# One decoder layer on one core: the memory's keys and values projected first, x made ready beside them

## The chip, the core and the metric

The kernel runs on one core of a Trainium2 chip. The metric is device microseconds (us) from start to end of one execution. The engines are PE (TensorE, matrix products and transposes), DVE (VectorE), ACT (ScalarE), POOL (GpSimd) and SP (SyncE, which here only issues DMAs). Engines run their own instruction queues in order and wait for each other by semaphores.

## What is computed

One hybrid decoder layer on 256 rows of width 2048, in float32. Cut to what matters here:

```python
x = x + 0.5 * swiglu_ffn(rmsnorm(x, g_ffn1), w_ffn1_gu, w_ffn1_down)      # d_ff 5632
h = rmsnorm(x, g_mix)
conv_in, cq, ckv, k_pe, mq, gate_logits = split(h @ w_in)
y_a = silu(layernorm(causal_conv31(glu(conv_in)))) @ w_conv_out
y_b = latent_attention(cq, ckv, k_pe) @ w_mla_out                         # 12 heads
mk, mv = split(rmsnorm(mem, g_mem) @ w_mem_kv, 2)                         # mem (256, 2048), 2 x 1024 columns
mk = rmsnorm(mk per head); mq = rmsnorm(mq per head)                      # 4 heads of 256
y_c = (softmax(mq mk^T / 16) mv) @ w_mem_out
x = x + (gates * (y_a, y_b, y_c)).sum() @ w_out
x = x + 0.5 * swiglu_ffn(rmsnorm(x, g_ffn2), w_ffn2_gu, w_ffn2_down)
```

The memory's keys and values depend on `mem`, `g_mem` and `w_mem_kv` alone, on nothing that the layer computes from x.

## The kernel before, in words

**Products.** Float32 is split into a high part of type fp32r and the rest: weights into `h` and `l` (`wh`, `wl` in the mixer), activations into `tH` and `tL` (plain), `xN` or `xsH`, `xsL` (forms). One product of tiles is three matmuls (`mul`, L497 to L499): high by high, low by high, high by low. The split of a weight chunk is a cast on ACT (L468, L199 in the mixer) and a subtraction on DVE (L469, L201).

**FFN stage.** The weights come in chunks of two K tiles by 2 x 512 columns (`pair_chunk`, L456: one chunk is 1 MB, two loads of 512 KB on SP's queue, three buffers in turn). Eight pairs make a block of gate and up (`PAIRS`). A plain pair (`eight`) takes eight tile products, 24 matmuls of 512 columns. In a block with forms, the pairs 0, 2 and 4 (`SEVEN`) take seven products, 21 matmuls, by a Strassen-like scheme: DVE adds weight tiles (L486), splits three more tiles (`t`, `th`, `tl`), and the activations need sums too (`seven_forms`, L505 to L507). `run_pairs` (L580) walks a list of such units, asks for the next chunk ahead, and calls a hook after each. A block's four sums stay in the four PSUM banks `acc`; four more banks (`misc`) hold transposes and the seven scheme's remainders.

**The start.** x comes in four blocks of 512 columns (`load_x`). The first block of gate and up is plain: x is turned with its gain but not its row norm (`block_T`, transposes at L270, tH at L252, tL at L253), and the norm is applied to the result. Meanwhile the squares of x are summed on ACT (L242), and after the fourth pair on, `prepare` scales x by its row norm (L632), turns it again (`pair_forms`, L527) and makes the forms for the other ten blocks. The hooks `mid` and `after` place these steps. Only the first chunk is loaded and split in four small pieces (`first`).

**The mixer.** `mixer` projects conv_in, then latents, rotary key and memory query from `w_in`, and then the memory's keys and values from `w_mem_kv` (`linear`, same three matmuls at L220 to L222): four column blocks of 16 K tiles, 384 matmuls of 512 columns. `memory_T` (L1070) loads the memory by POOL's queue, turns it and sums its squares shortly before. Then come the memory's attention (`mem_attention`, four heads in steps `turn`, `scores`, `probs`, `values` spread over the first gate blocks), the latent attention and the rest. The convolution is 360 steps on DVE (L1022); they fill what DVE has free.

**Order.** Steps that are not pinned are placed on each engine's queue by the framework's scheduler, by its own estimates; `pinned` steps keep the program's order, and until the first four units are through, so do the loads (`pin_dma`). `defer` holds a step back by a count of weight chunks, `until` and `flush` call it earlier.

Of the kernel before, what the change touches and what calls it, by code (L numbers as in the profile page):

```python
# [19 lines left out]
P = 128  # L20
# [56 lines left out]
class Layer:  # L77
    def __init__(self, ctx, tc, d, out):
# [14 lines left out]
        self.begin = True  # L93
# [362 lines left out]
    def pair_chunk(self, W3, pr, cs, seven, first=False):  # L456
# [123 lines left out]
    def run_pairs(self, units, after, end=None):  # L580


        def chunk(n):
            _, pr, seven, _, W3, cs, _ = units[n]
            w = self.pair_chunk(W3, pr, cs, seven, self.begin)
            self.begin = False
            return w

        w = chunk(0)
        for n, (q, pr, seven, forms, W3, cs, last) in enumerate(units):  # L590
# [11 lines left out]
            after(n, q)  # L602
# [10 lines left out]
    def ffn(self, W, blocks, xs, gain, rstd_, W_down, load, done, mid=None, between=None, end=None):  # L613
# [3 lines left out]
        get = self.xT_fn(blocks)  # L617

        def plain_forms(pr):
            r = []  # L620
            for k in range(2):
                h, l = get(2 * pr + k)
                r.append([(h[:, tt * P:tt * P + P], l[:, tt * P:tt * P + P]) for tt in range(2)])
            return r

        forms = {}

        def prepare(c):
            rstd = self.get(rstd_)
            xn = xs[c]  # L630
# [18 lines left out]
        units = []  # L649
        for b in range(NB):  # L650
            cs = slice(b * CB, (b + 1) * CB)
            if b == 0:
                q = self.lazy(lambda: self.quad(PAIRS, 0))
                units += [(q, pr, False, plain_forms, W3, cs, pr == PAIRS - 1) for pr in range(PAIRS)]
            else:
                q = self.lazy(lambda: self.quad(PAIRS - N7, N7))
                units += [(q, pr, pr in SEVEN, forms.__getitem__, W3, cs, pr == PAIRS - 1) for pr in range(PAIRS)]

        def after(n, q):
            b, pos = divmod(n, PAIRS)  # L660
            if b == NB:
                return down(pos, q)
            if b > NB:
                return down(n - NB * PAIRS, q)
            if b == 0:
                if mid is not None:
                    mid(pos)
                if PAIRS - 5 <= pos < PAIRS - 1:
                    prepare(pos - (PAIRS - 5))
# [6 lines left out]
            if b == 0:  # L676
# [19 lines left out]
            self.defer(4.0 * 6 - 1, lambda: turn(h))  # L696

# [627 lines left out]
```

## Time and profile before

| | |
|---|---|
| three runs | 2416.39, 2417.24, 2417.72 us; median 2417.24 |
| profiled execution | 2419.43 us, from its first to its last instruction (span) 2417.7 us |
| PE busy | 2396.8 us, 99% of the span |
| DVE busy | 1878.0 us, 78% |
| ACT busy | 1271.8 us, 53% |
| chain that ended last | 96% PE, 2% DVE, 1% ACT, 1% DMA |
| granted TensorE clock | 0.998 of full speed on average |

The busy time of PE counts the length of a matmul in the pipeline, so a stretch can read as busy while matmuls start late; counting instructions against the time of a stretch tells more. The chain is followed back from the last instruction, at each step to what released it.

### The profile page before, as it was taken

Reading aid. Unit: us, or ns where it says so; the run is one execution under the profiler, and the core shown is the slowest. Engines: PE = TensorE matmul, PEld = TensorE weight load, DVE = VectorE, ACT = ScalarE, POOL = GpSimd, SP = SyncE. Lnnn points to the kernel's source line nnn. Section 1 sums busy time; section 2 is a strip of 40 time slices with the busy share of each in tenths; the row PEclk is TensorE's granted clock in tenths of the full one; section 3 lists DMA queues with packets and bytes.
Section 4 is the critical chain, followed back from the end, with each engine's and each line's share of the span. In section 5 each row is a group of like instructions: output and inputs, shape, how many; then the busy total and the mean of one; then the engine's idle time right before and its main releaser. Section 6 shows DMA issues by size and latency. Waiting matters only on the chain.

```text
span 2417.7 us, 29511 instructions
## 1 busy us (share of the span) xinstructions
PE 2396.8 (99%) x10938; PEld 1987.0 (82%) x10938; DVE 1878.0 (78%) x2130; ACT 1271.8 (53%) x1452; POOL 84.2 (3%) x185
## 2 busy tenths in 40 slices
PE   8999999999999999999999999999999999999999
PEld 6788888888888889888888788888888888888887
DVE  5898888898875999975555576665688888888985
ACT  6655555455554555544556565345655555555543
POOL 1000000000000000000112100000000000000000
PEclk9999999999999999999999999999999999999999
DMA  6556555566567665664555557756555655566664
GB/s 221 175 184 212 200 197 195 205 218 217 193 221 234 184 185 181 183 195 139 172 162 164 166 174 218 235 183 205 195 192 192 206 194 194 205 204 215 207 201 149
DMA packets 224513, 469.94 MB, mean 194 GB/s; under 512 B 16304, under 2 KB 24096, under 8 KB 224368
## 3 DMA queue, kind: packets, MB, share of 16 engines
q1 hardware_dynamic: 218192, 449.90, 57.4%
q0 software_dynamic: 4992, 16.04, 2.0%
q10 hardware_dynamic: 1184, 2.11, 0.2%
q8 instruction: 86, 1.41, 0.2%
q14 instruction: 59, 0.48, 0.1%
HBM read 461.69 MB, written 6.29 MB: 194 GB/s over the span
## 4 chain that ended last, share of the span: by engine, by line
PE 96%; DVE 2%; ACT 1%; DMA 1%; issue 1%; SPq 0%; DVEq 0%; ACTq 0%
PE acc L498 15%; PE acc L497 15%; PE acc L499 15%; PE acc L220 12%; PE acc L222 12%; PE acc L221 12%; PE misc L497 3%; PE misc L499 3%; PE misc L498 3%; DVE l L469 1%; PE misc L645 1%; PE misc L270 1%; ACT h L468 1%; PE misc L1253 1%; PE misc L1252 0%
## 5 line engine op out<-in xcount | busy, mean ns | idle before, releaser
L468 ACT CAST h<-raw 128x2048 fp32r<-128x2048 f32 (+1 forms) x267 | 505.1, 1892 | 525.4 <-PE acc L498 274.8
L469 DVE TENSOR_TENSOR l<-raw,h 128x2048 fp32r<-128x2048 f32 (+1 forms) x267 | 604.6, 2265 | 190.9 <-ACT h L468 190.4
L201 DVE TENSOR_TENSOR wl<-raw,wh 128x1024 fp32r<-128x1024 f32 (+1 forms) x330 | 397.3, 1209 | 226.4 <-ACT wh L199 223.2
L199 ACT CAST wh<-raw 128x1024 fp32r<-128x1024 f32 (+1 forms) x330 | 342.7, 1042 | 389.8 <-PE acc L221 339.0
L497 PE MATMUL acc<-h,xN 128*128 128x512 f32 x1312 | 513.0, 391 | 0.0
L499 PE MATMUL acc<-l,xN 128*128 128x512 f32 x1312 | 511.1, 390 | 0.0
L498 PE MATMUL acc<-h,xN 128*128 128x512 f32 x1312 | 511.0, 389 | 0.0
L220 PE MATMUL acc<-wh,tH 128*128 128x512 f32 (+3 forms) x1088 | 422.2, 388 | 0.5 <-DVE gate L994 0.5
L222 PE MATMUL acc<-wl,tH 128*128 128x512 f32 (+3 forms) x1088 | 415.9, 382 | 0.0
L221 PE MATMUL acc<-wh,tL 128*128 128x512 f32 (+3 forms) x1088 | 415.4, 382 | 0.0
L499 PEld LDWEIGHTS acc<-l,xN 128*128 128x128 f32 x1312 | 246.4, 188 | 51.1
L497 PEld LDWEIGHTS acc<-h,xN 128*128 128x128 f32 x1312 | 246.5, 188 | 50.2
L498 PEld LDWEIGHTS acc<-h,xN 128*128 128x128 f32 x1312 | 246.5, 188 | 50.1
L220 PEld LDWEIGHTS acc<-wh,tH 128*128 128x128 f32 x1088 | 204.6, 188 | 39.6 <-issue 2.6
L222 PEld LDWEIGHTS acc<-wl,tH 128*128 128x128 f32 x1088 | 204.4, 188 | 38.8
L221 PEld LDWEIGHTS acc<-wh,tL 128*128 128x128 f32 x1088 | 204.8, 188 | 36.6
L486 DVE TENSOR_TENSOR t<-raw 128x1024 f32<-128x1024 f32 (+1 forms) x168 | 160.5, 955 | 14.3 <-DMA raw<-in_w_ffn_down_dram 9.3
L469 DVE TENSOR_TENSOR tl<-t,th 128x1536 fp32r<-128x1536 f32 x84 | 147.3, 1754 | 7.0 <-ACT th L468 4.5
L1022 DVE SCALAR_TENSOR_TENSOR y<-aT,cw,y 128x256 f32<-128x256 f32 x360 | 150.3, 476 | 0.0
L468 ACT CAST th<-t 128x1536 fp32r<-128x1536 f32 x84 | 124.8, 1486 | 43.4 <-PE acc L498 30.2
L497 PE MATMUL misc<-th,xsH 128*128 128x512 f32 x168 | 65.9, 392 | 3.8 <-ACT xf L530 3.8
L497 PE MATMUL misc<-h,xsH 128*128 128x512 f32 x168 | 66.5, 396 | 0.9 <-ACT xf L530 0.9
(287 smaller groups left out, 2765.6 us busy)
## 6 DMA issues: line engine op xcount, KB each, us to landing
raw<-in_w_ffn_gu_dram SPq DMA_DIRECT2D x290, 512.0 KB, 4.0
raw<-in_w_in_dram SPq DMA_DIRECT2D x172, 512.0 KB, 3.6
raw<-in_w_ffn_down_dram SPq DMA_DIRECT2D x152, 512.0 KB, 4.5
raw<-in_w_ffn_gu_dram SPq DMA_DIRECT2D x124, 256.0 KB, 4.0
raw<-in_w_mem_kv_dram SPq DMA_DIRECT2D x32, 512.0 KB, 3.8
raw<-in_w_out_dram SPq DMA_DIRECT2D x32, 512.0 KB, 3.6
raw<-in_w_ffn_down_dram SPq DMA_DIRECT2D x48, 256.0 KB, 4.8
raw<-in_w_conv_out_dram SPq DMA_DIRECT2D x24, 512.0 KB, 4.6
```

The source lines that it names most:

```text
L199: self.pinned(nc.scalar.copy(wh, raw))
L201: self.pinned(nc.vector.tensor_tensor(out=wl, in0=raw, in1=wh.bitcast(F32), op=ALU.subtract))
L220: nc.tensor.matmul(ps[tt], xh[:, t], wh[:, j, :], start=st, stop=False)
L221: nc.tensor.matmul(ps[tt], xl[:, t], wh[:, j, :], start=False, stop=False)
L222: nc.tensor.matmul(ps[tt], xh[:, t], wl[:, j, :], start=False, stop=sp)
L468: self.pinned(nc.scalar.copy(h[:, r], src[:, r]))
L469: self.pinned(nc.vector.tensor_tensor(out=l[:, r], in0=src[:, r], in1=h[:, r].bitcast(F32), op=ALU.subtract))
L486: add = lambda o, x, y: nc.vector.tensor_tensor(out=o, in0=x, in1=y, op=ALU.add)
L497: nc.tensor.matmul(ps, xh, wh, start=st, stop=False)
L498: nc.tensor.matmul(ps, xl, wh, start=False, stop=False)
L499: nc.tensor.matmul(ps, xh, wl, start=False, stop=sp)
L1022: nc.vector.scalar_tensor_tensor(out=y, in0=aT[ch // 3][:, ch % 3, k:k + S], scalar=self.cw[:, ch, k:k + 1], in1=y, op0=ALU.mult, op1=ALU.add)
```

## The change

The program now begins with the memory: `load_in` brings its four blocks, `turn_m` turns them with g_mem, and two plain runs of eight pairs (`plain_run`), keys then values, project it with the FFN stage's chunks and hooks (`mem_unit`). The result is scaled by the memory's row norm and written to DRAM (`kvd`); the keys' squares are summed at once. The four blocks of x are loaded after pairs 3 to 6 of the keys, their squares summed, and the forms of x are made after pairs 1, 3, 5 and 6 of the values. All eleven blocks of the first gate and up then use forms (`mixed_run`), so three of eight pairs in the first block are seven-product units; the second FFN keeps its plain first block. In the mixer, `memory_T` and the projection are gone; four loads on POOL's queue bring the keys and values back. The first chunk is still loaded and split in quarters; the second to the sixth are loaded as before and split in halves (`step`).

```diff
-    def pair_chunk(self, W3, pr, cs, seven, first=False):
+    def pair_chunk(self, W3, pr, cs, seven, step=4):
...
-                if first:
+                if step == 1:
                     for g in range(2):
                         self.pinned(nc.sync.dma_start(out=raw[:, 2 * i + g], in_=W3[k, g, cs]), self.pin_dma)
                 else:
                     self.pinned(nc.sync.dma_start(out=raw[:, 2 * i:2 * i + 2], in_=W3[k, :, cs]), self.pin_dma)
-            return split(raw, "hl", 4, 1 if first else 4)
+            return split(raw, "hl", 4, step)
...
-            _, pr, seven, _, W3, cs, _ = units[n]
-            w = self.pair_chunk(W3, pr, cs, seven, self.begin)
-            self.begin = False
-            return w
+            _, pr, seven, _, W3, cs, _, _ = units[n]
+            self.begun += 1
+            return self.pair_chunk(W3, pr, cs, seven, 1 if self.begun == 1 else 2 if self.begun < 7 else 4)
 
         w = chunk(0)
-        for n, (q, pr, seven, forms, W3, cs, last) in enumerate(units):
+        for n, (q, pr, seven, forms, W3, cs, last, after) in enumerate(units):
...
             w = nxt
             self.tick(4.0)
-            after(n, q)
+            after(q)
+
+    def plain_run(self, W3, cs, blocks, after):
+
+        get = self.xT_fn(blocks)
+
+        def forms(pr):
+            r = []
+            for k in range(2):
+                h, l = get(2 * pr + k)
+                r.append([(h[:, tt * P:tt * P + P], l[:, tt * P:tt * P + P]) for tt in range(2)])
+            return r
+
+        q = self.lazy(lambda: self.quad(PAIRS, 0))
+        return [(q, pr, False, forms, W3, cs, pr == PAIRS - 1, lambda q, pr=pr: after(pr, q)) for pr in range(PAIRS)]
+
+    def mixed_run(self, W3, cs, forms, after):
+        q = self.lazy(lambda: self.quad(PAIRS - N7, N7))
+        return [(q, pr, pr in SEVEN, forms.__getitem__, W3, cs, pr == PAIRS - 1,
+                 lambda q, pr=pr: after(pr, q)) for pr in range(PAIRS)]
+
+    def prepare(self, forms, xs, c, gain, rstd_):
+
+        rstd = self.get(rstd_)
+        for tt in range(2):
+            self.nc.scalar.activation(out=xs[c][:, tt], in_=xs[c][:, tt], func=AF.Identity, scale=rstd[:, tt:tt + 1])
+        for pr in (2 * c, 2 * c + 1):
+            forms[pr] = self.pair_forms(xs[c], pr, gain, pr in SEVEN)
 
     def lazy(self, make):
         got = []
...
+        mem_v = d["mem"].rearrange("(t p) c -> p t c", p=P)
+        ms, memT, xs, forms = [], [], [], {}
+        rmem, rstd = {}, {}
+        self.kvd = [self.dp.tile([P, 2, CB], F32, tag=f"kv{c}", name=f"kv{c}") for c in range(NCB)]
+        self.ssk = self.const([P, 2, 2, 2], name="ssmk")
+
+        def load_in(to, v, c):
             x = self.gen([2, CB], F32, "x")
-            n = CB // 2 if c == 0 else CB
+            n = CB // 2 if to is ms and c == 0 else CB
             for o in range(0, CB, n):
-                self.pinned(nc.sync.dma_start(out=x[:, :, o:o + n], in_=x_v[:, :, c * CB + o:c * CB + o + n]), True)
-            xs.append(x)
-
-        def turn_x(c):
-            blocks.append(self.block_T(xs[c], self.gains("g_ffn1", c), 0.0, 0.1))
-
-        def mid(pos):
+                self.pinned(nc.sync.dma_start(out=x[:, :, o:o + n], in_=v[:, :, c * CB + o:c * CB + o + n]), True)
+            to.append(x)
+
+        def turn_m(c):
+            memT.append(self.block_T(ms[c], lambda j: self.g_mem[:, 4 * c + j:4 * c + j + 1], 0.0, 0.1))
+
+        def mem_unit(g, pos, q):
+            n = PAIRS * g + pos
             self.pin = False
-            self.pin_dma = pos < 4
-            if pos < 3:
-                load_x(pos + 1)
-            if pos in (0, 2, 4):
-                turn_x(pos // 2 + 1)
-            if pos == 2:
-                self.stats(xs, D, 0.1, 0.1, True, rstd)
-
-        (self.g_ffn1,) = self.load_gains([d["g_ffn1"]], "g1", nc.scalar)
-        load_x(0)
-        turn_x(0)
+            self.pin_dma = n < 4
+            if n < 3:
+                load_in(ms, mem_v, n + 1)
+            if n in (0, 2, 4):
+                turn_m(n // 2 + 1)
+            if n == 2:
+                self.stats(ms, D, 0.1, 2.0, True, rmem)
+            if 3 <= n < 3 + NCB:
+                load_in(xs, x_v, n - 3)
+            if n == 6:
+                self.stats(xs, D, 0.1, 2.0, True, rstd)
+            if n in (9, 11, 13, 14):
+                self.prepare(forms, xs, {9: 0, 11: 1, 13: 2, 14: 3}[n], self.g_ffn1, rstd)
+            if pos < PAIRS - 1:
+                return
+            r = self.get(rmem)
+            kv = []
+            for c in range(2):
+                t = self.gen([2, CB], F32, "mkv")
+                kv.append(t)
+                for tt in range(2):
+                    nc.scalar.activation(out=t[:, tt], in_=q["F"][2 * c + tt], func=AF.Identity,
+                                         scale=r[:, tt:tt + 1])
+                nc.gpsimd.dma_start(out=self.kvd[2 * g + c], in_=t)
+            if g == 0:
+                for h in range(MEM_HEADS):
+                    self.defer(4.0 + 4 * h, lambda h=h: self.head_sumsq(self.ssk, kv, h))
+
+        self.g_ffn1, self.g_mem = self.load_gains([d["g_ffn1"], d["g_mem"]], "g1", nc.scalar)
+        load_in(ms, mem_v, 0)
+        turn_m(0)
+        W3 = d["w_mem_kv"].rearrange("k (h g f) -> k h g f", h=2, g=2)
+        units = []
+        for g in range(2):
+            units += self.plain_run(W3[:, g], slice(0, CB), memT, lambda pos, q, g=g: mem_unit(g, pos, q))
...
-        self.ffn(d["w_ffn1_gu"], blocks, xs, self.g_ffn1, rstd, d["w_ffn1_down"],
-                 residual(lambda c: x_v[:, :, c * CB:(c + 1) * CB]), done1, mid,
-                 (self.load_mixer, self.setup_mixer), end1)
+        units += self.ffn(d["w_ffn1_gu"], forms, d["w_ffn1_down"], residual(lambda c: x_v[:, :, c * CB:(c + 1) * CB]),
+                          done1, between=(self.load_mixer, self.setup_mixer))
+        self.run_pairs(units, end1)
...
-        memT, rmem = self.memory_T()
...
         kv = []
-        ssk = self.const([P, 2, 2, 2], name="ssmk")
-        for c in range(4):
-            ps = self.linear(d["w_mem_kv"], c * CB, CB, self.xT_fn(memT), KT)
-            r = self.get(rmem)
+        for c in range(NCB):
             t = self.gen([2, CB], F32, "mkv")
+            nc.gpsimd.dma_start(out=t, in_=self.kvd[c])
             kv.append(t)
-            for tt in range(2):
-                nc.scalar.activation(out=t[:, tt], in_=ps[tt], func=AF.Identity, scale=r[:, tt:tt + 1])
-            if c < 2:
-                for h in (2 * c, 2 * c + 1):
-                    self.defer(1.0 + h % 2, lambda h=h: self.head_sumsq(ssk, kv, h))
         self.flush()
-        omT = self.mem_attention(mq, kv[:2], kv[2:], ssq, ssk)
+        omT = self.mem_attention(mq, kv[:2], kv[2:], ssq, self.ssk)
 
         oT = [{"h": self.gen([4, S], F32R, "oH"), "l": self.gen([4, S], F32R, "oL"), "left": 0} for _ in range(3)]
         merged = [None] * NCB
...
+        units = []
+        for b in range(NB):
+            cs = slice(b * CB, (b + 1) * CB)
+            then = lambda pos, q, b=b: after(b, pos, q)
+            if b == 0 and blocks is not None:
+                units += self.plain_run(W3, cs, blocks, then)
+            else:
+                units += self.mixed_run(W3, cs, forms, then)
+
```

How the instructions lie now, at three places. **SP, the loads after the third chunk.** `raw` are weight chunks (two loads each), `x` blocks of x or, from `in_mem`, of the memory. Before:

```order
L479 DMA raw_257<-in_w_ffn_gu_dram 128x2x512 x2
L772 DMA x_288<-in_x_dram 128x2x512
L479 DMA raw_302<-in_w_ffn_gu_dram 128x2x512 x2
L479 DMA raw_394<-in_w_ffn_gu_dram 128x2x512 x2
L479 DMA raw_466<-in_w_ffn_gu_dram 128x2x512 x2
```

With the change:

```order
L479 DMA raw_267<-in_w_mem_kv_dram 128x1024 x2
L778 DMA x_300<-in_mem_dram 128x2x512
L479 DMA raw_314<-in_w_mem_kv_dram 128x1024 x2
L479 DMA raw_420<-in_w_mem_kv_dram 128x1024 x2
L778 DMA x_364<-in_x_dram 128x2x512
L479 DMA raw_366<-in_w_mem_kv_dram 128x1024 x2
L479 DMA raw_468<-in_w_mem_kv_dram 128x1024 x2
L479 DMA raw_553<-in_w_mem_kv_dram 128x1024 x2
L479 DMA raw_502<-in_w_mem_kv_dram 128x1024 x2
```

`raw_366` is the sixth chunk, `raw_420` the seventh: the seventh is issued first, with a block of x between them; the ninth and tenth (`raw_502`, `raw_553`) are exchanged too.

**ACT, the first casts.** `h` are the casts of weight chunks, `tH` the turned activations, two K tiles from each `misc`. Before:

```order
L252 ACTIVATE tH_124<-misc_126,g_17_119 128x256 x2
L468 CAST h_148<-raw_143 128x512 x4
L468 CAST h_165<-raw_162 128x2048
L252 ACTIVATE tH_124<-misc_193,g_17_119 128x256
L468 CAST h_218<-raw_215 128x2048
L252 ACTIVATE tH_124<-misc_193,g_17_119 128x256
```

With the change:

```order
L252 ACTIVATE tH_130<-misc_132,g_18_125 128x256 x2
L468 CAST h_154<-raw_149 128x512 x4
L468 CAST h_171<-raw_168 128x1024 x2
L252 ACTIVATE tH_130<-misc_201,g_18_125 128x256
L468 CAST h_226<-raw_223 128x1024 x2
L252 ACTIVATE tH_130<-misc_201,g_18_125 128x256
```

The second and third chunks (`h_171`, `h_226`) are cast in halves; the third and fourth K tile's tH keep their places behind them.

**DVE, one head of the memory's attention.** `mx`, `nmx`, `rs` and `me` are its softmax, `wl` weight splits, `y` steps of the convolution. Before:

```order
L1132 TENSOR_REDUCE mx_8239<-misc_8234 128x2
L1134 TENSOR_TENSOR nmx_8241<-mx_8239,mnsq_8105 128x2
L1141 RECIPROCAL rs_8247<-sm_8244 128x2
L1143 TENSOR_SCALAR me_8243<-me_8243,rs_8247 128x256 x2
L201 TENSOR_TENSOR wl_8400<-raw_8396,wh_8398 128x1024
```

With the change:

```order
L1142 TENSOR_REDUCE mx_8282<-misc_8277 128x2
L1043 SCALAR_TENSOR_TENSOR y_6188<-aT_6184,cw_1572,y_6188 128x256
L1144 TENSOR_TENSOR nmx_8284<-mx_8282,mnsq_8003 128x2
L1043 SCALAR_TENSOR_TENSOR y_6188<-aT_6184,cw_1572,y_6188 128x256
L1043 SCALAR_TENSOR_TENSOR y_6188<-aT_6185,cw_1572,y_6188 128x256
L1043 SCALAR_TENSOR_TENSOR y_6189<-aT_6185,cw_1572,y_6189 128x256 x2
L1151 RECIPROCAL rs_8290<-sm_8287 128x2
L1043 SCALAR_TENSOR_TENSOR y_6189<-aT_6186,cw_1572,y_6189 128x256
L1153 TENSOR_SCALAR me_8286<-me_8286,rs_8290 128x256 x2
L201 TENSOR_TENSOR wl_8434<-raw_8430,wh_8432 128x1024
```

Before, the convolution was through ahead of this; now six of its steps lie between the steps of the softmax.

## Rows read from the trace of the kernel before

**Rows 1.** The page: busy us, share and instructions of each engine
```profile
PE 2396.8 (99%) x10938; PEld 1987.0 (82%) x10938; DVE 1878.0 (78%) x2130; ACT 1271.8 (53%) x1452; POOL 84.2 (3%) x185
```

**Rows 2.** Two stretches: engines' busy time, PE clock, DMA share, GB/s
```profile
core 0: us, PE busy (x) PEld busy (x) DVE busy (x) ACT busy (x) POOL busy (x), PEclk, DMA share, GB/s
149.40:191.80 42.40, 42.40 (x192) 35.20 (x191) 37.93 (x33) 22.16 (x16) 0.00 (x0) 1.00 0.59 199
880.00:1060.00 180.00, 180.00 (x900) 153.77 (x899) 175.73 (x331) 98.83 (x165) 9.04 (x12) 1.00 0.61 185
```

**Rows 3.** The chain of waits, in order of time: start us, us, what
```profile
150.51 0.88 PE misc L645 x8
```

**Rows 4.** Stretch from third chunk to hidden block, columns as above
```profile
26.80:106.78 79.98, 72.34 (x330) 57.67 (x329) 60.12 (x64) 57.31 (x81) 8.53 (x17) 0.98 0.48 163
```

**Rows 5.** PE's transposes in that stretch: xcount, busy us, mean ns
```profile
L527 PE MATMUL misc<-ident,x 128*128 128x128 f32 x32 | 4.8, 275 | 0.0
...
L270 PE MATMUL misc<-ident,x 128*128 128x128 f32 x19 | 3.1, 275 | 1.7 <-ACT xf L530 1.7
```

**Rows 6.** Waits of PE in that stretch: total us, times, longest us
```profile
PE misc L497 <- ACT xf L530: 4.2, 2, 3.8
```

**Rows 7.** Two stretches of 10 us, columns as in rows 2
```profile
10.00:20.00 10.00, 7.18 (x27) 5.14 (x27) 2.69 (x3) 4.21 (x4) 0.00 (x0) 0.88 1.03 385
...
50.00:60.00 10.00, 7.12 (x36) 5.15 (x35) 9.78 (x14) 9.46 (x19) 5.75 (x12) 1.00 0.69 231
```

**Rows 8.** The timeline: start us, us, instruction [idle before <-releaser]
```profile
13.95 1.90 ACT L468 CAST h<-raw 128x2048 fp32r<-128x2048 f32 x1 [5.01 <-DMA raw<-in_w_ffn_gu_dram]
...
15.33 0.66 PE L270 MATMUL misc<-ident,x 128*128 128x128 f32 x4 [0.92 <-DMA x<-in_x_dram]
15.75 0.47 ACT L252 ACTIVATE tH<-misc,g 128x256 fp32r<-128x256 f32 x1
...
18.07 1.90 ACT L468 CAST h<-raw 128x2048 fp32r<-128x2048 f32 x1 [1.85 <-DMA raw<-in_w_ffn_gu_dram]
18.09 0.48 DVE L253 SCALAR_TENSOR_TENSOR tL<-misc,g,tH 128x256 fp32r<-128x256 f32 x1
...
26.82 0.48 PE L497 MATMUL acc<-h,tH 128*128 128x512 f32 x1
```

**Rows 9.** DVE and ACT, 0 to 110 us: xcount, busy us, mean ns
```profile
L469 DVE TENSOR_TENSOR l<-raw,h 128x2048 fp32r<-128x2048 f32 x16 | 36.7, 2291 | 18.2 <-ACT h L468 18.2
...
L632 ACT ACTIVATE x<-x,r 128x512 f32<-128x512 f32 x8 | 5.3, 722 | 0.0
...
L469 DVE TENSOR_TENSOR tl<-t,th 128x1536 fp32r<-128x1536 f32 x3 | 5.3, 1754 | 1.0 <-ACT th L468 1.0
...
L486 DVE TENSOR_TENSOR t<-raw 128x1024 f32<-128x1024 f32 x4 | 4.9, 1222 | 0.0
...
L250 DVE TENSOR_TENSOR xN<-xf,xN 128x512 fp32r<-128x512 f32 x5 | 3.4, 687 | 0.7 <-ACT xN L249 0.7
...
L505 DVE TENSOR_TENSOR xf<-xf 128x256 f32<-128x256 f32 x3 | 1.3, 424 | 0.5 <-ACT xf L530 0.5
...
L506 DVE TENSOR_TENSOR xf<-xf 128x128 f32<-128x128 f32 x3 | 0.9, 288 | 0.0
```

**Rows 10.** Page: costliest groups (busy, mean ns), weights' issues (us to landing)
```profile
L201 DVE TENSOR_TENSOR wl<-raw,wh 128x1024 fp32r<-128x1024 f32 (+1 forms) x330 | 397.3, 1209 | 226.4 <-ACT wh L199 223.2
L199 ACT CAST wh<-raw 128x1024 fp32r<-128x1024 f32 (+1 forms) x330 | 342.7, 1042 | 389.8 <-PE acc L221 339.0
...
L1022 DVE SCALAR_TENSOR_TENSOR y<-aT,cw,y 128x256 f32<-128x256 f32 x360 | 150.3, 476 | 0.0
...
raw<-in_w_ffn_gu_dram SPq DMA_DIRECT2D x290, 512.0 KB, 4.0
```

**Rows 11.** The timeline of one head's softmax in the memory's attention
```profile
1074.28 0.62 DVE L1143 TENSOR_SCALAR me<-me,rs 128x256 f32<-128x256 f32 x2
...
1078.24 0.60 PE L1151 MATMUL misc<-ident,me 128*128 128x128 f32 x4
```

More of the change, by code (lines that the diff above doesn't have):

```diff
@@ L92, in __init__ @@
         self.pin = True
-        self.begin = True
+        self.begun = 0
     def ffn_stage(self):
@@ L359, in setup_mixer @@
         nc, d = self.nc, self.d
-        (self.g_mix, self.g_ffn2, self.g_mem, self.ln_g, self.ln_b, self.cv_b, self.g_q_a, self.g_kv_a,
+        (self.g_mix, self.g_ffn2, self.ln_g, self.ln_b, self.cv_b, self.g_q_a, self.g_kv_a,
          gqn, gkn, gmq, gmk) = self.turn_rows(*self.rows, "gains")
@@ L578, in remainders, with run_pairs @@
         v.tensor_tensor(out=e[1][:, 1], in0=e[1][:, 0], in1=p7, op=ALU.add)
-    def run_pairs(self, units, after, end=None):
+    def run_pairs(self, units, end=None):
         def chunk(n):
-            _, pr, seven, _, W3, cs, _ = units[n]
-            w = self.pair_chunk(W3, pr, cs, seven, self.begin)
-            self.begin = False
-            return w
+            _, pr, seven, _, W3, cs, _, _ = units[n]
+            self.begun += 1
+            return self.pair_chunk(W3, pr, cs, seven, 1 if self.begun == 1 else 2 if self.begun < 7 else 4)
         w = chunk(0)
-        for n, (q, pr, seven, forms, W3, cs, last) in enumerate(units):
+        for n, (q, pr, seven, forms, W3, cs, last, after) in enumerate(units):
             q, f = q(), forms(pr)
@@ L611, in lazy, with ffn @@
         return get
-    def ffn(self, W, blocks, xs, gain, rstd_, W_down, load, done, mid=None, between=None, end=None):
+    def ffn(self, W, forms, W_down, load, done, blocks=None, xs=None, gain=None, rstd_=None, between=None):
         nc = self.nc
         W3 = W.rearrange("k (g f) -> k g f", g=2)
[L617 to L630, printed above, removed]
-            for tt in range(2):
-                nc.scalar.activation(out=xn[:, tt], in_=xn[:, tt], func=AF.Identity, scale=rstd[:, tt:tt + 1])
-            for pr in (2 * c, 2 * c + 1):
-                forms[pr] = self.pair_forms(xn, pr, gain, pr in SEVEN)
         hT = []
@@ L648, in ffn, with after @@
         NB = D_FF // CB
[L649 to L669, printed above, removed]
+        def after(b, pos, q):
+            if b == 0 and blocks is not None and PAIRS - 5 <= pos < PAIRS - 1:
+                self.prepare(forms, xs, pos - (PAIRS - 5), gain, rstd_)
             if b == NB - 1:
@@ L724, in ffn @@
             q = q0 if g == 0 else q1[half]
-            units += [(q, half * HALF + p, p in SEVEN, hid.__getitem__, V, slice(0, CB),
-                       p == HALF - 1 and r != 1) for p in range(HALF)]
+            units += [(q, half * HALF + p, p in SEVEN, hid.__getitem__, V, slice(0, CB), p == HALF - 1 and r != 1,
+                       lambda q, m=r * HALF + p: down(m, q)) for p in range(HALF)]
         def down(m, q):
@@ L745, in down @@
                     done(2 * g + c, y)
-        self.run_pairs(units, after, end)
+        return units
     def finish_stats(self, ss, dim):
@@ L837, in done2 @@
                 nc.scalar.dma_start(out=out_v[:, tt, c * CB:(c + 1) * CB], in_=x[:, tt])
-        self.ffn(d["w_ffn2_gu"], blocks, xs, self.g_ffn2, rstd, d["w_ffn2_down"], residual(lambda c: xd2[c]), done2)
+        self.run_pairs(self.ffn(d["w_ffn2_gu"], {}, d["w_ffn2_down"], residual(lambda c: xd2[c]), done2,
+                                blocks, xs, self.g_ffn2, rstd))
         self.slots.close()
@@ L1068, in conv @@
         return yT
-    def memory_T(self):
-        nc, d = self.nc, self.d
-        mem_v = d["mem"].rearrange("(t p) c -> p t c", p=P)
-        blocks, ms = [], []
-        for c in range(NCB):
-            m = self.gen([2, CB], F32, "mem")
-            nc.gpsimd.dma_start(out=m, in_=mem_v[:, :, c * CB:(c + 1) * CB])
-            ms.append(m)
-            blocks.append(self.block_T(m, self.gains("g_mem", c), 6.0 + 5 * c, 2.5))
-        return blocks, self.stats(ms, D, 6.0, 5.0)
     def head_sumsq(self, ss, tiles, h):
```

8 lines of the change are left out of this document (2 added, 6 removed).

## The prediction

> **What bounds the kernel now.** I read the page first, then a stretch in mid FFN, then the first 110 us, then the mixer. The page has PE busy for 2396.8 us, 99% of the span [rows 1]: PE is the bound, and a change pays if it takes instructions from PE or ends a wait of PE. The steady stretch gives prices: one block of gate and up takes 42.40 us at full clock [rows 2], and 8 transposes take 0.87 us on the chain [rows 3]. The block has 183 products of 512 columns and 8 transposes, so a transpose is 0.109 us and a product (42.40 - 0.87) / 183 = 0.227 us. (The rows of single products show about 0.39 us; that is their length in the pipeline, their starts lie 0.227 apart.)
>
> Where PE loses time is the start. From the first product of the third weight chunk (26.8) to the first transpose of a hidden block (106.78) it issues 330 instructions in 79.98 us [rows 4]; 32 + 19 of them are transposes [rows 5]. That is 279 x 0.227 + 51 x 0.109 = 68.9 us of work: 11.1 us are lost. The longest wait is 3.8 us, for a form of x [rows 6], and DVE is busy 9.78 of 10 us from 50 to 60 [rows 7]. So the second half of the first block, which must make the forms of x and split the first seven-product weights, is bound by DVE, which begins it with nothing in hand. Earlier, the second chunk's 24 products stretch from 15.33 to 26.82, behind a DMA, a cast and a tL [rows 8], at a clock that is at half (1.2 GHz) for a part [rows 7].
>
> I call one pair of K tiles with its weights a unit: 24 products, or 21 with seven forms. Before: u0 to u7 are the plain first gate and up. After: u0 to u7 and u8 to u15 are the two halves of the memory's projection, and gate and up begin at u16.
>
> **Work taken off PE.** The memory's 384 products stay plain and only change place: nothing gained, 87 us (384 x 0.227) move from the mixer to the front. The first gate and up now has three seven-product units, 9 products less: 9 x 0.227 = 2.0 us. x was turned twice, plain at L270 and for the forms at L527 (32 transposes [rows 5]), and the memory once in the mixer; now each is turned once: 32 x 0.109 = 3.5 us. PE's work is hidden by nothing, so **5.5 us** go.
> The Trainium skill (TensorE: Matmul & The Clock Gate, section Back-to-back issue gap) gives a warm stream N / 2.4 GHz + 2.5 ns, as an estimate 56 ns for 128 columns and 216 ns for 512; by that page this term would be 1.8 + 1.9 = 3.7 us. The rows above, 109 and 227 ns, disagree, and they decide.
>
> **The start, up to the third chunk.** The small pieces split casts and subtractions, not loads (but for the first, as before). ACT got all of u1 at 13.95 [rows 8]; at the 385 GB/s of that stretch [rows 7] half of it, 0.5 MB, takes 1.36 us, so the first half is there at 12.6. Half a cast is 1.04 us, half a subtraction 1.21 [rows 10]; tH and tL take 0.47 and 0.48 [rows 8]. The second half is cast at 15.0, the third K tile's tH is out at 15.5, l at 16.2, tL at 16.7. PE's queue still has four transposes ahead that a DMA releases at 15.33 [rows 8]. The fourth K tile's tH now stands behind both halves of u2, landed by 18.07 [rows 8]: cast 19.1, tH 19.6, tL 20.1. Then 12 products and 4 transposes: u2 starts at 23.2 with full clock instead of 26.8, 3.6 us earlier. If the clock falls as it did, some ten products cost double: 25.5, 1.3 us earlier. The two ends differ by the clock alone; two of the three idle spells ahead of the old fall remain, so I take the end near that row: **1.3 us**.
> g_mem is one more small DMA on ACT ahead of PE's first transpose, about 0.5 us later; the wait for the DMA at 15.33 swallows it: nothing.
>
> **The stall from 40 to 75 us.** The forms of x are now made at u9 to u14, beside plain units, where DVE has little to do. By the rows of DVE [rows 9], the forms of one block cost at most 0.42 + 2 x 0.29 + 3 x 0.69 = 3.1 us (three blocks) or 1.4 (the last), 10.7 in all. Eight plain chunks cost 8 x 2.29 = 18.3; a seven chunk 1.22 + 2 x 0.69 + 2.29 + 1.75 = 6.6, so u16 to u18 cost 15.5. Together 44.5 us. PE needs from the start of u8 to that of u18 8 x 5.44 + 3.5 + 4.8 + 5.4 = 57 us. DVE is 12 us ahead where it used to be behind: all **11.1 us** go. What is late next: the second half's sums need the banks that ACT empties of the first (0.72 us each, as L632 [rows 9]), and these are finished 1.36 us apart (6 products), so it fits. Tightest is u7, whose last tL I find ready some 0.8 us before PE: nothing, at most 1 us.
>
> **The queues in the first 50 us.** SP now issues u6's loads ahead of u5's, with a block of x between (rows of the order above). They wait for u3's subtraction, by the same walk at about 25.9. The first half MB lands 4.0 us after its issue [rows 10], the other four at 1.36 each: u5 is there at 35.3, cast by 37.5, subtracted by 39.5. PE reaches u5 at 40.8 (u2 at 23.2, then three units of 5.44 and 12 transposes): hidden, by 1.3 us. x's 2 MB more take the queue 5.4 us within eight units of 5.44 us, whose own 8 MB take it 22: hidden. POOL writes keys and values and reads them back; it issues the reads after the second latent's norm, with the projections of rotary key and query (1088 columns, 46 us of PE) still ahead of their first use: hidden.
>
> **The mixer.** Its PE work shrinks by 87 us while the convolution keeps its 360 steps of 476 ns on DVE [rows 10]. DVE is busy 175.7 of 180 us there and PE never waits [rows 2]. The convolution now reaches in between the steps of the memory's softmax (order above). Before, one head's probabilities are ready at 1074.9 and PE turns them at 1078.24: 3.3 us in hand [rows 11]. Two convolution steps on that chain add 1.0 us: nothing. If DVE runs 3 us behind besides, 0.7 us for each of four heads: 3 us at most.
>
> **Sum.** 5.5 + 1.3 + 11.1 = 17.9 us. The profiled execution took 2419.43 us (its span 2417.7), 2.19 over the median 2417.24 of the three runs; taken from the median, **2399.3 us**. Best 2417.24 - 20.2 = 2397.0; with the 1 and 3 us paid 2403.3.
>
> **Rivals.**
> (a) *The DVE stall only moves*, to u16 to u23: first forms and first seven chunks still meet. For it: a steady block leaves DVE little (37.9 of 42.4 us [rows 2]), so a lag is not made up. Against it: the 12 us. The 11.1 us stay: 2410.4.
> (b) *u5 comes late*: its loads leave behind u6 and x, its casts behind u6's. It decides if PE is over 1.3 us earlier, or a load later, than in the walk; then u5 waits about as long as u6's cast and subtraction take (1.9 [rows 8] and 2.3), and a clock at half adds some 1.8: 6 us, 2405.3.
> (c) *Slower*: the memory's attention among convolution steps. Four heads with four steps are 16 places where PE waits in order; if each waits for four steps, 1.9 us, that is 30 us: 2430. It makes the kernel slower from (17.9 + 4.8) / 16 = 1.4 us per place. Against it: the 3.3 us.
> (d) *The small pieces do nothing*: the fourth tH alone decides u1, and u2 starts at 26.8 as before: 2400.6, within the forecast's range.
>
> **How the numbers follow.** Forecast with (d) 0.65 (own range 2396 to 2403.5), (b) 0.16, (a) 0.12, (c) 0.05, none of these 0.02. From 2396 (1 us under the best sum, for what the bounds miss) to 2408 lie the forecast and (b): 0.81. About 0.2%, 4.8 us, is what a measurement can tell from no change. Forecast, (a) and (b) are faster by more, less a little for sums that fail together: 0.92; slower 0.05; same 0.03.
>
> **What would show it.** Right: no PE wait over 1 us from 27 to 150 us; DVE under 9 of 10 us while u8 to u15 run; and from u2 on PE at the prices above. The clock from 10 to 30 us tells which end u1 took. Wrong: a PE wait for h or l near 40 us (b), for xsL or tl near 105 to 130 us (a), for me, mqk or mkv among the first gates (c).

## The result, and the profile after

The changed kernel took 2401.99 us (median of 4 runs, 2400.95 to 2403.93), the kernel before 2417.48 (4 runs): ratio 0.9938, 95% interval 0.992 to 0.9955, so 15.5 us faster. A second set of runs gave 2400.62 against 2417.43, ratio 0.9931 (0.9918 to 0.9945), 16.8 us. The forecast was 2399.3 us (17.9 faster), its range 2396 to 2408. The profiled execution of after took 2400.95 us, its span is 2399.2; that of before 2417.7, so this pair differs by 18.5.

The page, engines (answers to [rows 1]: PE has 41 instructions and 12.0 us less):

```profile
PE 2384.8 (99%) x10897; PEld 1979.1 (82%) x10897; DVE 1884.4 (79%) x2122; ACT 1265.5 (53%) x1429; POOL 90.8 (4%) x188
```

All waits of PE from 0 to 200 us of after (columns as in [rows 6], whose wait of 4.2 us answers to the third line):

```profile
PE misc L342 <- DMA rows<-in_g_mem_dram: 6.1, 1, 6.1
PE acc L497 <- ACT h L468: 1.3, 1, 1.3
PE misc L497 <- ACT xf L530: 0.5, 1, 0.5
PE acc L498 <- DVE tL L253: 0.3, 1, 0.3
```

The stretch from the third chunk (u2) to the first transpose of a hidden block, columns as in [rows 4], and the product with which u2 starts (timeline):

```profile
23.30:178.63 155.33, 154.47 (x705) 127.45 (x704) 112.50 (x102) 103.49 (x143) 11.11 (x22) 1.00 0.67 225
```
```profile
23.31 0.48 PE L497 MATMUL acc<-h,tH 128*128 128x512 f32 x1
```

By the prediction's prices these 705 instructions (654 products, 51 transposes) are 654 x 0.227 + 51 x 0.109 = 154.0 us of work: 1.3 us are lost where 11.1 were [rows 4]. u2 starts at 23.3 in place of 26.8 [rows 8], the granted clock is 1.00 all the way. PE waits 6.1 us for its first instruction, on the small load of g_mem; before, its first product came 2.7 us earlier, at 6.95 against 9.62.

### The profile page after: what moved, and what is told of

It reads as the page before. It is cut to its first block, busy times and chain, and to the rows that moved or that the text cites. A ratio compares the mean times of both kernels' runs of the same rounds, so it can differ in the third digit from the quotient of the medians.

```text
span 2399.2 us, 29402 instructions
## 1 busy us (share of the span) xinstructions
PE 2384.8 (99%) x10897; PEld 1979.1 (82%) x10897; DVE 1884.4 (79%) x2122; ACT 1265.5 (53%) x1429; POOL 90.8 (4%) x188
## 4 chain that ended last, share of the span: by engine, by line
PE 98%; DVE 1%; ACT 0%; DMA 0%; issue 0%; ACTq 0%; DVEq 0%
PE acc L498 17%; PE acc L497 17%; PE acc L499 17%; PE acc L220 11%; PE acc L222 11%; PE acc L221 11%; PE misc L499 3%; PE misc L497 3%; PE misc L498 3%; PE misc L655 1%; PE misc L270 1%; PE misc L1263 1%; PE misc L1262 0%; PE misc L527 0%; PE misc L1139 0%; PE misc L1171 0%
## 5 line engine op out<-in xcount | busy, mean ns | idle before, releaser
L468 ACT CAST h<-raw 128x2048 fp32r<-128x2048 f32 (+2 forms) x288 | 536.3, 1864 | 545.6 <-PE acc L498 270.0
L469 DVE TENSOR_TENSOR l<-raw,h 128x2048 fp32r<-128x2048 f32 (+2 forms) x288 | 641.9, 2230 | 203.8 <-ACT h L468 203.0
L497 PE MATMUL acc<-h,xN 128*128 128x512 f32 x1352 | 528.0, 391 | 0.0
L498 PE MATMUL acc<-h,xN 128*128 128x512 f32 x1352 | 526.1, 389 | 0.0
L201 DVE TENSOR_TENSOR wl<-raw,wh 128x1024 fp32r<-128x1024 f32 (+2 forms) x298 | 360.5, 1216 | 195.0 <-ACT wh L199 193.7
L199 ACT CAST wh<-raw 128x1024 fp32r<-128x1024 f32 (+2 forms) x298 | 308.4, 1041 | 341.0 <-PE acc L221 290.0
L220 PE MATMUL acc<-wh,tH 128*128 128x512 f32 (+3 forms) x960 | 371.4, 387 | 0.5 <-DVE gate L1015 0.5
L222 PE MATMUL acc<-wl,tH 128*128 128x512 f32 (+3 forms) x960 | 365.6, 381 | 0.0
L221 PE MATMUL acc<-wh,tL 128*128 128x512 f32 (+3 forms) x960 | 365.1, 380 | 0.0
L497 PE MATMUL acc<-h,tH 128*128 128x512 f32 x192 | 76.8, 401 | 1.3 <-ACT h L468 1.3
L498 PE MATMUL acc<-h,tL 128*128 128x512 f32 x192 | 75.6, 394 | 0.3 <-DVE tL L253 0.3
```

Source lines behind the costliest of these rows:

```text
L199: self.pinned(nc.scalar.copy(wh, raw))
L201: self.pinned(nc.vector.tensor_tensor(out=wl, in0=raw, in1=wh.bitcast(F32), op=ALU.subtract))
L220: nc.tensor.matmul(ps[tt], xh[:, t], wh[:, j, :], start=st, stop=False)
L221: nc.tensor.matmul(ps[tt], xl[:, t], wh[:, j, :], start=False, stop=False)
L222: nc.tensor.matmul(ps[tt], xh[:, t], wl[:, j, :], start=False, stop=sp)
L468: self.pinned(nc.scalar.copy(h[:, r], src[:, r]))
```

## Two profiles of each: where the time went

The executions that were profiled lie 1 to 2 us beside their medians, so both kernels were run and profiled again.

**c_before**: the kernel before, unedited.

> The kernel before, not edited, for a second profile of it. The first one took 2419.4 us, 2.0 over the median 2417.4. If its start was typical, u2 again starts at 26.8 us, with the granted clock at half for some 7 us between 17 and 25 us, and the losses from 40 to 80 us again sum to 11 us. If it was an unlucky one, u2 starts 1 to 2 us earlier and the clock stays at 1.00 there; the 11 us from 40 to 80 stay in either case.

2417.07 us (11 runs, 2415.84 to 2417.99; ratio to the other runs of before 0.9998, 0.9989 to 1.0007), span 2416.2. Its start (timeline and two stretches), the stretch of [rows 4] and ten us within it:

```profile
23.93 0.48 PE L497 MATMUL acc<-h,tH 128*128 128x512 f32 x1
```
```profile
17.00:20.00 3.00, 2.37 (x10) 1.99 (x11) 1.57 (x3) 2.64 (x3) 0.00 (x0) 1.00 1.05 388
20.00:24.00 4.00, 3.47 (x18) 2.58 (x16) 2.56 (x4) 0.47 (x1) 0.00 (x0) 1.00 1.03 370
23.92:105.13 81.21, 75.09 (x330) 59.73 (x329) 58.72 (x64) 57.47 (x81) 8.54 (x17) 0.94 0.52 171
50.00:60.00 10.00, 7.11 (x26) 5.12 (x25) 9.70 (x17) 9.45 (x17) 7.63 (x15) 0.70 0.75 237
```

The first profile of before was an unlucky one at the start: here u2 comes 2.9 us earlier and the granted clock stays at 1.00 there. The stall is back, and larger: 81.21 - 68.9 = 12.3 us. Part of it is the clock, which is down within the stall (0.70 of full speed from 50 to 60 us, last line; 1.00 there in the first profile [rows 7]).

**a0_same**: the changed kernel, unedited.

> The changed kernel again, not edited, as the scale for the others and to see how much executions differ. Expected: 2402.0 us, within 1.5 us; in its profile PE starts its first transpose at 6.1 us and its first product at 9.6, the third chunk (u2) at 23.3, and no wait of PE from 27 to 150 us is longer than 0.6 us. If executions differ in the start, as the granted clock of before (half from 17.6 to 24.4 us) suggests, this profile shows u2 at another place or a clock under 1.00 between 10 and 30 us.

2400.62 us (5 runs, 2400.49 to 2400.70), span 2398.8; PE's first instruction at 5.0, u2 at 22.84; the same stretch:

```profile
22.83:178.43 155.60, 154.53 (x705) 127.45 (x704) 112.45 (x102) 103.53 (x143) 11.14 (x22) 1.00 0.68 225
```

It loses 155.60 - 154.0 = 1.6 us. The terms of the forecast beside both pairs of profiles (the last line is what remains of the difference of the spans):

```
us                                   forecast   first pair              second pair
start to u2                             1.3     26.82 - 23.31 =  3.5    23.93 - 22.84 =  1.1
stall, u2 to the hidden block          11.1     11.1 - 1.3    =  9.8    12.3 - 1.6    = 10.7
work off PE, and all else               5.5     18.5 - 13.3   =  5.2    17.4 - 11.8   =  5.6
sum                                    17.9                     18.5                    17.4
```

## Experiments on the start

**a1_whole**: only the very first chunk in small pieces.

```diff
-return self.pair_chunk(W3, pr, cs, seven, 1 if self.begun == 1 else 2 if self.begun < 7 else 4)
+return self.pair_chunk(W3, pr, cs, seven, 1 if self.begun == 1 else 4)
```

> The changed kernel with only the very first chunk in small pieces, u1 to u5 cast and subtracted whole as before the change. Theory 1 (the pieces bring the third chunk forward, as in the forecast's walk): u2 starts 1.3 to 3.6 us later than 23.3, so 2403.3 to 2405.6 us. Theory 2 (the late g_mem holds PE back until 9.6 us, so that u1 is ready in time either way): whole, u1 is cast from 12.3 to 14.2 and subtracted by 16.5, u2's cast ends at 18.9 and the fourth K tile's tL at 19.9, while PE asks for u1 at 17.4 and for the fourth K tile at 20.1; u2 at 23.3 to 24, 2402 to 2402.7 us.

2401.13 us (2400.73 to 2403.13), ratio to before 0.9935 (0.9923 to 0.9948); u2 at 23.19. Theory 2: in the changed kernel the small pieces move nothing that can be measured. PE has no wait for tL at the start.

**b1_before_pieces**: the same pieces in the kernel before (a count in place of its flag for the first chunk).

```diff
-w = self.pair_chunk(W3, pr, cs, seven, self.begin)
+w = self.pair_chunk(W3, pr, cs, seven, 1 if self.begun == 1 else 2 if self.begun < 7 else 4)
```

> The kernel before with the first chunks in the changed kernel's small pieces (u1 to u5 in halves) and nothing else. Theory 1 (the pieces bring u2 forward where PE is there early and waits, as in the kernel before): tL of the third K tile at 16.7 us in place of 18.6, no half clock, u2 1.3 to 3.6 us earlier: 2413.8 to 2416.1 us. Theory 2 (the pieces do nothing, as in the changed kernel with whole chunks, 2401.1 against 2400.6): 2417.4, within 1 us. In both the stall from 40 to 80 us stays within 2 us of its 11.

2416.02 us, ratio 0.9995 (0.9986 to 1.0003). Its u2 starts at 22.45, 1.5 us before that of c_before, and its span is 2414.1 against 2416.2. So where PE is at the second chunk early and waits, the pieces do what the forecast's walk said, though the runs can't tell the 1.0 us from nothing. After the change there is no such wait left for them.

**a2_gains**: g_mem's row first and alone, g_ffn1's row turned after u5. **b3_gains_pin**: besides, the fourth K tile's tH ahead of u2's casts on ACT.

```diff
-self.g_ffn1, self.g_mem = self.load_gains([d["g_ffn1"], d["g_mem"]], "g1", nc.scalar)
+(self.g_mem,) = self.load_gains([d["g_mem"]], "g1", nc.scalar)
+late = self.load_rows([d["g_ffn1"]], nc.scalar)
...
+            if n == 5:
+                (self.g_ffn1,) = self.turn_rows(*late, "g2")
```
```diff
-            self.pin = False
+            self.pin = n < 1
```

> The changed kernel with g_mem's row loaded first and turned alone, g_ffn1's row turned behind u5: PE's first instruction no longer waits for two small loads. First transpose at 4.1 to 4.5 us in place of 5.0 to 6.1, first product at 7.2 in place of 8.5 to 9.6, u1 asked for at 15.2. Theory 1 (the late g_mem is the whole price): all of it, 1.6 us, reaches the end: 2399.0. Theory 2 (the fourth K tile's tH, behind u2's two casts whose halves land at 14.4 to 17.0 us, is next): PE waits for its tL until 17.9 to 19.4 us, u2 0.3 to 1.7 us earlier than 22.8: 2398.9 to 2400.3, with a wait of PE for tL from 17 to 20 us; if the clock falls behind this wait, up to 2402.

> As the run before, and the fourth K tile's tH kept ahead of u2's casts on ACT. u2 at 21.2 us, 1.6 earlier than the 22.8 of the changed kernel's second profile, with no wait of PE for tL from 15 to 22 us: 2399.0 us by both theories; by theory 2 of the run before it is faster than that run by 0 to 1.4 us (or 3, if the clock fell there), by theory 1 it is the same.

2400.04 us (2398.80 to 2400.19), ratio 0.9927, and 2399.46 (2398.91 to 2400.48), ratio 0.9926: the two are the same. PE begins at 3.5 and 3.2 us, but the first product comes at 8.11 and 8.27, not at 7.2, and the wait is another one (waits of PE, 0 to 200 us, of b3_gains_pin):

```profile
PE misc L342 <- POOL invf L393: 3.2, 1, 3.2
PE acc L497 <- ACT h L468: 2.2, 1, 2.2
PE misc L270 <- DMA x<-in_mem_dram: 0.6, 1, 0.6
PE misc L497 <- ACT xf L530: 0.5, 1, 0.5
```

The late g_mem stood almost wholly in front of a wait that was there anyway, the one for the first weights: in a2_gains their cast starts as soon as the load has landed (timeline), and that is 0.36 us before the cast in a0_same (7.80 us).

```profile
7.44 0.62 ACT L468 CAST h<-raw 128x512 fp32r<-128x512 f32 x1 [0.52 <-DMA raw<-in_w_mem_kv_dram]
```

By the medians g_mem cost 0.6 and 1.2 us (against the 2400.62 of a0_same), not 2.7. The pinned tH brought nothing: u2 starts at 22.01 in a2_gains and, where 21.2 was expected, at 22.98 in b3_gains_pin, where more of the first products run at half rate (13, against 8). No wait for tL showed in either run.

**e1_warm**: b3_gains_pin with 14 transposes of the identity that nobody reads.

```diff
+warm(6)
 (self.g_mem,) = self.load_gains([d["g_mem"]], "g1", nc.scalar)
 load_in(ms, mem_v, 0)
 turn_m(0)
+warm(8)
```

> As the kernel with g_mem first and the fourth tH ahead of u2's casts (2399.5), with 14 transposes of the identity that nobody reads: six before PE's first real instruction, eight between the first two groups of four. PE is then busy from 2 to 8 us. Theory 1 (the products of the first chunk are at half rate, 13 of them 0.43 us apart in that kernel's profile, because PE idled and had only begun; work ahead of them brings the full clock earlier): under 6 products 0.43 us apart, u1 asked for 1 to 2 us earlier, of which the third K tile's tL, ready at 14.8, takes back what lies beyond 1.5: 2398.0 to 2398.8. Theory 2 (the clock rises at the same time whatever PE does before): 2399.5, with 13 slow products as before.

The first products of b3_gains_pin and of e1_warm (timeline):

```profile
8.86 0.63 PE L498 MATMUL acc<-h,tL 128*128 128x512 f32 x1
9.29 0.63 PE L497 MATMUL acc<-h,tH 128*128 128x512 f32 x1
9.72 0.63 PE L498 MATMUL acc<-h,tL 128*128 128x512 f32 x1
```
```profile
9.03 0.40 PE L497 MATMUL acc<-h,tH 128*128 128x512 f32 x1
9.27 0.40 PE L498 MATMUL acc<-h,tL 128*128 128x512 f32 x1
```

0.43 us apart there (13 of them), 0.24 here (none at 0.43): with PE at work from 1.6 us on, the half rate of the first chunk is gone, and u2 starts at 21.17 in place of 22.98: theory 1, for the rate. Yet the median is 2400.59 (2398.04 to 2401.48), not the 2398.0 to 2398.8 of theory 1, and no gain that can be told. The profiled execution, one of the longer ones, lost most of it again far from the start (timeline; PE waits for a subtraction of the second FFN's hidden forms):

```profile
2162.83 0.50 PE L498 MATMUL misc<-h,xsL 128*128 128x512 f32 x1 [1.15 <-DVE xsL L250]
```

This wait of about 1 us is in the profile of a3_bunch too and in none of after, a0_same and b3_gains_pin: one source of the 1 to 3 us by which executions differ, and it has nothing to do with the change.

## Experiments on the stall

**a3_bunch**: the four blocks of x prepared behind u11 to u14, one unit after the other.

```diff
-            if n in (9, 11, 13, 14):
-                self.prepare(forms, xs, {9: 0, 11: 1, 13: 2, 14: 3}[n], self.g_ffn1, rstd)
+            if n in (11, 12, 13, 14):
+                self.prepare(forms, xs, n - 11, self.g_ffn1, rstd)
```

> The changed kernel with the four blocks of x prepared in four units on end, behind u11 to u14 (as before the change, when they stood behind u3 to u6, two units ahead of the first seven-product unit), in place of u9, u11, u13 and u14. Theory 1 (the stall went because DVE has eight plain units more in which to get ahead, 12 us by the forecast's sum): within 1 us of the changed kernel, 2401 to 2403. Theory 2 (the stall went because the forms are spread over more units): up to 11.1 us of it come back, in waits of PE for xsL, xsH or tl between 85 and 130 us: 2406 to 2413.

2401.31 us (2399.32 to 2402.78), ratio 0.9933: theory 1. That the forms are spread over more units is not what ended the stall; at the spacing of before, ahead of the first unit with seven products, it stays away. One thing the run leaves together: before the change the plain transposes of x stood among those of the forms, now the plain ones are the memory's and are over by then.

**b4_forms_last**: the first block behind u13, the other three behind u15.

```diff
-            if n in (9, 11, 13, 14):
-                self.prepare(forms, xs, {9: 0, 11: 1, 13: 2, 14: 3}[n], self.g_ffn1, rstd)
+            for c in {13: (0,), 15: (1, 2, 3)}.get(n, ()):
+                self.prepare(forms, xs, c, self.g_ffn1, rstd)
```

> The changed kernel with the first block of x prepared behind u13 and the other three behind u15, the last plain unit, so that their forms (7.6 us of DVE by the forecast's prices) stand among the first seven-product chunks. Theory 1 (head start): by the start of u20 DVE has to do some 31 us of work after u15 begins, PE gives it 26, and it has part of the chunks in hand: 0 to 5 us lost, 2402 to 2407. Theory 2 (any meeting of first forms and first seven chunks stalls PE, as rival (a) has it): 5 to 11 us lost, 2407 to 2413, with DVE busy over 9.7 of 10 us from 100 to 130 us.

2409.42 us (2408.61 to 2412.29), ratio 0.997 (0.9959 to 0.9981): 8.8 us of the gain given back, the size of theory 2, but not its mechanism. The waits of PE for xf from 0 to 200 us and two stretches of 10 us:

```profile
PE misc L527 <- ACT xf L530: 4.1, 2, 3.4
PE misc L497 <- ACT xf L530: 1.4, 2, 0.9
```
```profile
100.00:110.00 10.00, 5.67 (x35) 4.35 (x33) 7.10 (x10) 6.12 (x11) 0.00 (x0) 0.96 0.56 169
110.00:120.00 10.00, 8.76 (x28) 6.38 (x29) 4.53 (x9) 9.09 (x18) 1.64 (x4) 0.70 0.24 92
```

DVE is not full (7.1 and 4.5 of 10 us), and the weights of the first seven-product unit are ready long before. PE waits for **misc banks**: the seven scheme takes all four of them for its extra sums, and the transposed x sits in them until ACT has made xf of it. In ACT's queue that step stands behind casts of forms, which wait for DVE's sums of forms, which stand behind a subtraction of 2.29 us, which had itself waited for ACT (timeline):

```profile
104.10 2.29 DVE L469 TENSOR_TENSOR l<-raw,h 128x2048 fp32r<-128x2048 f32 x1 [1.89 <-ACT h L468]
...
106.76 0.29 DVE L506 TENSOR_TENSOR xf<-xf 128x128 f32<-128x128 f32 x1
...
107.09 1.03 ACT L249 CAST xsH<-xf 128x384 fp32r<-128x384 f32 x2 [2.28 <-DVE xf L506]
...
108.02 0.83 ACT L530 ACTIVATE xf<-misc,g 128x256 f32<-128x256 f32 x2
...
108.91 0.90 PE L527 MATMUL misc<-ident,x 128*128 128x128 f32 x4 [3.39 <-ACT xf L530]
```

The same is seen in the stall of before (timeline; the second line is the end of the split of the first seven-product weights, which is ready at 66.4), with the stretch from 70 to 80 us:

```profile
54.93 0.66 PE L270 MATMUL misc<-ident,x 128*128 128x128 f32 x4 [1.71 <-ACT xf L530]
...
64.68 1.75 DVE L469 TENSOR_TENSOR tl<-t,th 128x1536 fp32r<-128x1536 f32 x1
...
68.62 2.29 DVE L469 TENSOR_TENSOR l<-raw,h 128x2048 fp32r<-128x2048 f32 x1
...
70.34 0.39 PE L499 MATMUL misc<-tl,xsH 128*128 128x512 f32 x1
...
70.83 0.29 DVE L507 TENSOR_TENSOR xf<-xf 128x128 f32<-128x128 f32 x1
...
71.20 0.62 ACT L249 CAST xsH<-xf 128x512 fp32r<-128x512 f32 x1 [1.94 <-DVE xf L507]
...
73.60 0.83 ACT L530 ACTIVATE xf<-misc,g 128x256 f32<-128x256 f32 x2
...
74.48 0.50 PE L497 MATMUL misc<-th,xsH 128*128 128x512 f32 x1 [3.76 <-ACT xf L530]
```
```profile
70.00:80.00 10.00, 5.82 (x18) 3.82 (x17) 7.61 (x11) 8.67 (x14) 0.00 (x0) 0.83 0.56 193
```

PE uses tl at 70.34, 3.9 us after it is ready, and then stops for the next bank until ACT's xf at 73.60 has emptied it. Counted as time between the starts of PE's instructions, less their prices, the banks cost 1.9 us at 53 us (first line) and 4.5 at 70 to 76. Another 1.6 go to the half clock right behind (0.83 of full speed from 70 to 80 us), and 2.3 to plain waits for an h, a tH and a tL: some 10 of the 11.1. And in after, what is left of it at u16 (DVE, ACT and PE by the timeline):

```profile
92.90 1.75 DVE L469 TENSOR_TENSOR tl<-t,th 128x1536 fp32r<-128x1536 f32 x1
...
105.67 1.91 ACT L468 CAST h<-raw 128x2048 fp32r<-128x2048 f32 x1 [1.51 <-PE acc L498]
...
108.00 0.83 ACT L530 ACTIVATE xf<-misc,g 128x256 f32<-128x256 f32 x2
...
108.88 0.50 PE L497 MATMUL misc<-h,xsH 128*128 128x512 f32 x1 [0.52 <-ACT xf L530]
```

DVE has u16's last split done at 94.65 and PE uses it at 106.15, two products after u16's start: 11.5 us in hand. (The forecast's 12 is another count, DVE's work against PE's time up to u18, so the nearness of the two proves nothing.) Only the last block's bank is late, behind a weight cast that itself waited for PE.

**e3_shift** and **e2_warm_shift**: the forms one unit earlier, in b3_gains_pin and in e1_warm.

```diff
-            if n in (9, 11, 13, 14):
-                self.prepare(forms, xs, {9: 0, 11: 1, 13: 2, 14: 3}[n], self.g_ffn1, rstd)
+            if n in (8, 10, 12, 13):
+                self.prepare(forms, xs, {8: 0, 10: 1, 12: 2, 13: 3}[n], self.g_ffn1, rstd)
```

> The kernel with g_mem first and the fourth tH ahead of u2's casts (2399.5), with the forms one unit earlier and no identity transposes: 2398.8 if the bank of the last forms is what PE waited for at 107 us; with the two runs before it tells the share of each.

> As the run before, and the four blocks of x prepared one unit earlier (behind u8, u10, u12, u13), so that ACT has emptied the banks of the last forms before u16 asks for all four of them. The wait of PE for xf at 107 us (0.5 us, and 0.68 lost) goes: 0.7 us faster than the run before, 2397.3 to 2398.1. If the wait is for another thing than the bank of the last forms, it stays and the time is the same.

2398.82 us (2397.88 to 2399.28), ratio 0.9921 (0.9907 to 0.9934), and 2398.71 (2398.31 to 2399.71), ratio 0.9922. All waits of PE from 0 to 200 us of e3_shift:

```profile
PE misc L342 <- DMA rows<-in_g_mem_dram: 4.1, 1, 4.1
PE acc L497 <- ACT h L468: 1.6, 1, 1.6
PE misc L270 <- DMA x<-in_mem_dram: 0.2, 1, 0.2
```

The wait at u16 is gone, so it was the bank, and no wait of PE is left from 9 to 200 us. The first median is the one expected, the second lies 0.6 us over its range: the identity transposes bring nothing that the medians show. These two medians are the lowest, 1.8 and 1.9 us under the changed kernel's second set; their intervals overlap with its interval, so the version is better by the profile's count rather than by the runs.

## Why the prediction was right, and where its steps were off

**Work off PE, 5.5 us: right.** The two pairs leave 5.2 and 5.6 us for it and everything else, and PE has the 32 transposes and 9 products less that were counted. The trace's own prices held (the row of the eight transposes says 0.88 us, not 0.87, which changes nothing). The estimate by the formula of the Trainium skill (TensorE: Matmul & The Clock Gate, section Back-to-back issue gap) was 3.7 us and lies under both. That section gives the formula for the isolated gap of single matmuls, not for a warm stream; for a stream it names some 81 and 131 ns, as an estimate 2.6 + 1.2 = 3.8 us here, which the trace's 109 and 227 ns contradict as well.

**The stall, 11.1 us: right in size within 1.3 us, right in what ended it, short by a link in how it stops PE.** 9.8 and 10.7 us went. That DVE gets ahead during eight more plain units is borne out by the 11.5 us in hand, and by a3_bunch, where the old spacing did no harm. What the prediction left out is the bank: it said that PE was late because DVE splits the first seven-product weights late, and those were ready 3.9 us early. At 70 us a full DVE holds ACT, ACT holds the banks, the banks hold PE; at 53 us ACT, 9.46 of 10 us busy [rows 7], holds them by itself. Rival (a), as it was told, looks at DVE alone. b4_forms_last comes nearest to it and costs 8.8 us without a full DVE: what counts there is that the forms are out of the banks before u16 begins.

One of the prediction's signs failed: DVE was to be under 9 of 10 us while u8 to u15 run, and from 90 to 100 us it is at 9.91 (after; 9.75 in a0_same), while PE does not wait:

```profile
90.00:100.00 10.00, 10.00 (x53) 8.40 (x52) 9.91 (x11) 6.67 (x11) 0.00 (x0) 1.00 0.39 134
```

A full DVE that works ahead of PE costs nothing here, so that sign could not tell the stall. Of the two small waits that remain, u7's last tL was named ("nothing, at most 1 us"): 0.3 and 0.6 us waited. The other, at u16 (0.5 waited, 0.7 lost), was not: the banks of which the prediction says "it fits" are the four `acc` between keys and values, where PE indeed does not wait, and not the `misc` banks.

**The start, 1.3 us: the size right in the second pair (1.1), the reason wrong, so the match is luck.** The walk laid it to the small pieces, with PE at 6.95 us as before. In the changed kernel the pieces do nothing (a1_whole). Of rival (d) that premise is true; its reason, the fourth tH, and its consequence, u2 at 26.8, are not. PE itself begins late, for g_mem, whose cost the forecast put at 0.5 us and had swallowed by a wait for x; PE's first instruction came 1.7 to 2.9 us later than before. And when it came, u1 and u2 were ready and no gap was left in which the clock could fall: 3.5 us against the first profile of before, where it fell, 1.1 against the second, where it did not. Why they were ready is open. In a1_whole u1's cast, whole as before the change, starts when its load has landed, at 12.05 us, against 13.95 [rows 8] and 12.94 in the two profiles of before; no run separates these earlier loads from the late PE.

**The mixer, nothing: right.** The convolution's steps did move in among the memory's attention, and DVE there went from 59.6 to 101.1 of 110 us (before, then after):

```profile
1060.00:1170.00 110.00, 110.00 (x519) 93.03 (x518) 59.61 (x78) 54.58 (x88) 4.22 (x5) 1.00 0.53 159
```
```profile
1040.00:1150.00 110.00, 109.52 (x516) 92.16 (x515) 101.09 (x193) 53.48 (x85) 5.84 (x6) 1.00 0.55 166
```

PE lost 0.5 us in one wait for the probabilities `me`, and in a0_same no such wait is listed. Rival (c) needed 1.4 us at each of 16 places. Rival (b), u5 late, did not show: no wait for u5 is among PE's waits.

**The total.** 17.9 was forecast, the spans differ by 18.5 and 17.4, the medians by 15.5 and 16.8: by the medians the forecast is 1.1 to 2.4 us too large. The two that differ most come from the scatter of single executions: the profiled before was 2.0 us over its median, the profiled after 1.0 under.

## What to carry to other kernels

When two stretches of work compete for one engine at the start, put ahead of them work that depends on neither: during eight plain units, which ask DVE for 2.29 of every 5.44 us, it got 11.5 us in hand, and the spacing of the disputed work no longer mattered as long as that work ended before u16. Look for the resource that passes the wait on: busy engines stopped PE here mostly through four PSUM banks, and moving the last user of a bank one unit earlier took that wait away without less work on any engine. And check a gain at the start against a second profile of the kernel before: 2.4 of the 3.5 us that the first pair showed there are the difference between executions.

## What was not expected of the hardware

The first products run at half rate (0.43 us apart, 7 of them in after, 11 in a0_same, 13 in b3_gains_pin) although the granted clock reads 1.00 from the first us on; with transposes ahead of them that nobody reads, none does (e1_warm).

Like waits need not have like effects on the clock. In both profiles of before PE waits 1.7, 0.4 and 0.8 us for a bank, a tH and a tL, in the first from 53 to 58 us and in the second from 50 to 55; in the first the granted clock stays at 1.00 there, in the second it falls to half for some 6 us (0.70 from 50 to 60). So a good start was given back in part: the second lacks the fall from 17.6 to 24.4 us and starts u2 2.9 us earlier, but its stall is 1.2 us longer and the spans differ by only 1.5.
